# Low parts of a recurrent mixer's second low-rank matrices, from 64 rows to 128 rows with zeros below

## The chip, the core and the metric

One core of a Trainium2 chip runs the whole program. The metric is the device time of one execution in microseconds; for the kernel before it is the median of three executions.

## The reference, cut to what matters

The reference is a trunk of two layers on 256 context and 512 latent tokens of width 1024. Layer 0 is a linear recurrent mixer, layer 1 a recurrent mixer with a state matrix per head (16 heads of 64); each is followed by a mixture of 64 experts. The change is in layer 1. There the decay and the step size of every channel come from two low-rank products, in both directions z:

```
def _rwkv_prep(u, mu, w_in, w0, w_l1, w_l2, a0, a_l1, a_l2, ...):
    ...
    d_w = w0 + einsum('zbtl,zld->zbtd', tanh(einsum('btd,zdl->zbtl', xm[3], w_l1)), w_l2)
    w = exp(-RWKV_DECAY_SCALE * sigmoid(d_w))
    a = sigmoid(a0 + einsum('zbtl,zld->zbtd', einsum('btd,zdl->zbtl', xm[4], a_l1), a_l2))
    ...
```

The inner rank l is 64. `w_l2` and `a_l2` are the second low-rank matrices, 64 x 1024 each for the two directions.

## The kernel before, in words

Layer 1's mixer is the method `rwkv`. Its first stage computes keys, receptances, the gate and the hidden activations of the two low-rank products. The second stage, where the change lies, goes over eight channel blocks `j` of 128 channels (two heads). It runs from about 1600 us to 2475 us of the span.

Numbers are carried as pairs of parts, hi and lo, in the type fp32r, whose sum is the fp32 value. The hidden activations `hid[n][z]` (n is "w" or "a") are tiles of 128 rows by 768 tokens: rows 0 to 63 hold the hi part of the 64 hidden values, rows 64 to 127 the lo part. For each block, `loads` (L1429) fetches the 64 x 2 x 128 slices of the second matrices, and `key` (L1440) splits them: the hi part is written by ScalarE (L1447) into both halves of a tile of 128 rows, the lo part by VectorE (L1448) into a tile of 64 rows. In `a0` (L1465) each of six units (direction z, group g of 256 tokens) then makes for "w" and for "a" one pair of TensorE products of 256 columns: L1474 takes hi against all 128 rows of `hid` (that is hi times hi plus hi times lo), and L1475 adds lo against the 64 upper rows (lo times hi). The tile is called `l_ps` in the trace, the matrices `l2w` and `l2a`. Eight blocks, six units and two matrices give 96 such pairs. ScalarE reads each result with a tanh (L1476).

After `a0` come `a1` to `a5`: elementwise work, the score products `sc_ps` (L1535, 64 rows each, the two heads in rows 0 to 63 and 64 to 127) and the transposes `bt_ps` (L1568, 128 rows). `solver`, `inverse` and `merge` invert small triangular systems, with products of 32 x 32 (`pz`, L1631 and L1636). `chain` (L1647) is the recurrence itself: in twelve chunks, in both directions, `c0` (L1683), `c1` (L1697) and `c2` (L1708) form a serial loop from TensorE to ScalarE or VectorE and back, with products `pg` of 128 rows by 64 columns; `po` (L1718, L1720) gives the outputs. Beside it run the value projection of the blocks (`vproj`, `vp_ps`, L1343, 128 x 128), and the modulation of the next layer (`ada_ps`, L362).

The work of all blocks is put into one list of timed events (`at`, L1793, with the table SCH) and the closures are called in that order. The order on each engine is not that of the calls alone: the program is opened with `tile.TileContext(nc, schedule_with_timeline_sim=True)`, so the builder sets the order of instructions on each engine by a simulated timeline. TensorE takes its instructions strictly in the order that is set.

Of the kernel before, what the change touches and what calls it, by code (L numbers as in the profile page):

```python
# [9 lines left out]
F32 = mybir.dt.float32  # L10
F32R = mybir.dt.float32r
# [3 lines left out]
OP = mybir.AluOpType  # L15
# [256 lines left out]
class Kern:  # L272
# [789 lines left out]
    def rwkv(self, first, done, prepare, res):  # L1062
        nc, ins, tc = self.nc, self.ins, self.tc
# [4 lines left out]
        with ExitStack() as st:  # L1068
# [28 lines left out]
            hid = {n: [fr.tile([128, NTOK], F32R, name=f"hid{n}{z}") for z in range(2)] for n in "wa"}  # L1097
# [6 lines left out]
            with ExitStack() as s1:  # L1104
# [18 lines left out]
                for t in range(NT):  # L1123
                    h = first(t)
                    ps = psw.tile([128, KD, 128], F32, name="u1_ps", tag="w")
# [47 lines left out]
                def wload(ap, n):  # L1173

                    w = wp.tile([128, KD, n], F32, name="rw_f", tag=f"rwf")
                    self.load(w, ap.rearrange("(k p) n -> p k n", p=128))
                    hl = [wp.tile([128, KD, n], F32R, name=f"rw{s}", tag=f"rw{s}") for s in range(2)]
                    for k in range(0, KD, 2):
                        self.split(hl[0][:, k:k + 2], hl[1][:, k:k + 2], w[:, k:k + 2])
                    return hl  # L1180

                def proj_t(w, x, t0):

                    ps = psw.tile([128, 2, 512], F32, name="pt_ps", tag="w")
                    for k in range(KD):
                        for a, b in ((0, 0), (0, 1), (1, 0)):
                            for s, s0, n in SEGS:
                                if s0 >= t0:
                                    nc.tensor.matmul(ps[:, s, :n], w[a][:, k, :], x[k][b][:, s0:s0 + n],  # L1189
                                                     start=(k == 0 and a == 0 and b == 0), stop=(k == KD - 1 and a == 1))  # L1190
                    return ps
# [33 lines left out]
                for j in range(KD):  # L1225
                    w = wload(ins["rwkv_w_in"][0, 1][:, j * 128:(j + 1) * 128], 128)
                    ps = proj_t(w, x, 0)
# [21 lines left out]
                for j in range(KD):  # L1249
                    w = wload(ins["rwkv_w_in"][0, 0][:, j * 128:(j + 1) * 128], 128)  # L1250
                    ps = proj_t(w, x, NCTX)
# [5 lines left out]
                w = wload(ins["rwkv_g_l1"][0], 128)  # L1257
                ps = proj_t(w, x, NCTX)
# [9 lines left out]
                for t in range(NLAT // 128):  # L1268
                    ps = psw.tile([128, 2, 512], F32, name="gg_ps", tag="w")
                    for c in range(2):  # L1270
                        for n, (a, b) in enumerate(((0, 0), (0, 1), (1, 0))):
                            nc.tensor.matmul(ps[:, c, :], ghs[a][:, t * 128:(t + 1) * 128], g2s[b][:, c * 512:(c + 1) * 512],
                                             start=(n == 0), stop=(n == 2))
# [9 lines left out]
            with ExitStack() as s2:  # L1283
                b2 = sf.enter_context(self.pool(name="r2", bufs=1))
                pp = sf.enter_context(self.pool(name="r2_p", bufs=2))
# [143 lines left out]
                def loads(j, P):  # L1429
# [6 lines left out]
                    for n in "wa":  # L1436
                        w = P["l2f"][n] = pp.tile([64, 2, 128], F32, name=f"l2{n}", bufs=1)
                        self.load(w, ins[f"rwkv_{n}_l2"][0][:, :, J].rearrange("z l d -> l z d"))

                def key(j, P):  # L1440
                    P["l2"] = {}
                    for n in "wa":
                        w = P["l2f"][n]
                        hi = pp.tile([128, 2, 128], F32R, name=f"l2{n}0", bufs=1)
                        lo = pp.tile([64, 2, 128], F32R, name=f"l2{n}1", bufs=1)
                        for b in range(2):
                            nc.scalar.activation(hi[r64(b)], w, AF.Copy)  # L1447
                        nc.vector.tensor_tensor(lo, w, hi[:64].bitcast(F32), op=OP.subtract)  # L1448
                        P["l2"][n] = hi, lo

                    kk = P["kk"] = pp.tile([128, NTOK], F32, name="kk")
                    q = PO["kk"] + j
                    for s, t0, n in SEGS:
                        ps = psg.tile([128, 512], F32, name="kk_ps", tag="g")
                        nc.tensor.matmul(ps[:, :n], indT[:, j, :], rn[:, t0:t0 + n], start=True, stop=True)
                        nc.vector.scalar_tensor_tensor(kk[:, t0:t0 + n], P["kT"][:, t0:t0 + n], pc[:, q:q + 1], ps[:, :n], op0=OP.mult, op1=OP.mult)
                    P["kts"] = pp.tile([128, NLAT], F32, name="kts", bufs=1)

                    P["n_d"] = dp.tile([96, 32, 32], F32, name="n_d", bufs=4)
                    P["z_d"] = dp.tile([96, 32, 32], F32, name="z_d", bufs=4)  # L1460
                    P["no"] = wk.tile([128, NCH, 32], F32, name="no", bufs=BUF["no"])
# [3 lines left out]
                def a0(j, P, z, g):  # L1465
                    U = P[z, g] = {}
                    G = slice(256 * g, 256 * g + 256)
                    ps = psg.tile([128, 2, 256], F32, name="l2_ps", tag="g")
                    U["w"] = wk.tile([128, 256], F32, name="uw")
                    U["a"] = wk.tile([128, 256], F32, name="ua")  # L1470
                    for i, n in enumerate("wa"):
                        col = (i * 2 + z) * KD + j
                        hi, lo = P["l2"][n]
                        nc.tensor.matmul(ps[:, i, :], hi[:, z, :], hid[n][z][:, G], start=True, stop=False)  # L1474
                        nc.tensor.matmul(ps[:, i, :], lo[:, z, :], hid[n][z][:64, G], start=False, stop=True)  # L1475
                        nc.scalar.activation(U[n], ps[:, i, :], AF.Tanh, scale=0.5, bias=hb[:, col:col + 1])  # L1476

                def a1(j, P, z, g):
# [325 lines left out]
                for j in range(KD):  # L1804
                    P, t = {}, j * SCH["per"] + SCH["sh"][j]
                    at(t + SCH["ld"], lambda j=j, P=P: loads(j, P))
                    at(t + SCH["key"], lambda j=j, P=P: key(j, P))
                    for u, (z, g) in enumerate(UNITS):
                        for s, f in enumerate((a0, a1, a2, a3, a4, a5)):
                            at(t + SCH["a"] + SCH["du"] * u + SCH["ds"] * s, lambda f=f, a=(j, P, z, g): f(*a))  # L1810
                    t += SCH["off"][j]
                    so = solver(j, P)
                    for i, f in enumerate(so):
                        at(t + SCH["so"] + i * SCH["dso"], f)
                    at(t + SCH["so"] + 1, lambda j=j, P=P: bonus(j, P))
                    for z in range(2):
                        at(t + SCH["inv"] + z * 0.3, lambda a=(j, P, z): inverse(*a))
                    for i, (z, g) in enumerate(UNITS):
                        at(t + SCH["mo"][i], lambda a=(j, P, z, g): merge(*a))
                    b, c = chain(j, P)  # L1820
                    at(t + SCH["bt"], b)
                    for i, f in enumerate(c):
                        at(t + i, f)
                    for f, d in zip(readout(j, P), SCH["ro"]):
                        at(t + 36 + d, f)
# [14 lines left out]
                i = 0  # L1840
# [294 lines left out]
```

## Time and profile before

| | us |
|---|---|
| median of three executions | 3397.05 |
| lowest, highest | 3382.0, 3406.42 |
| the profiled execution | 3397.3 |
| its span, first to last instruction | 3395.5 |
| stage of the change, in the span | about 1600 to 2475 |

A row of the profile names an engine (PE is TensorE's products, PEld its weight loads, DVE VectorE, ACT ScalarE, POOL GpSimd), a line of the kernel, an operation and its tiles, out<-in. For TensorE "64\*128 64x256" means weights of 64 rows by 128 columns and a moving operand of 64 rows by 256 columns. The ends of products are modelled, starts are recorded, so the time a product takes of TensorE is read from its start to the next start. [...]

### The profile page before, as it was taken

How to read it: one execution, taken by the hardware profiler on the slowest of the kernel's cores; microseconds unless marked ns; L12 is line 12 of the kernel's file. 1: busy time of each engine (PE TensorE's matmuls, PEld its weight loads, DVE VectorE, ACT ScalarE, POOL GpSimd, SP SyncE). 2: the span in 40 equal slices, each digit the busy share in tenths (PEclk: the TensorE clock that was granted, in tenths of full speed). 3: DMA queues.
4: the chain of work that ended last, by engine and by line, in shares of the span. 5: the costliest groups of instructions: out<-in, count | busy, mean ns of one | idle time of the engine just before them, and what ended most of it. 6: DMA issues, size and time to landing. Idle time of an engine off the chain costs nothing. (4 is left out here: it accounts for less than half of the span.)

```text
span 3395.5 us, 52648 instructions
## 1 busy us (share of the span) xinstructions
PE 2976.2 (88%) x17929; PEld 2076.3 (61%) x17929; DVE 2403.6 (71%) x4728; ACT 2006.7 (59%) x3835; POOL 1125.8 (33%) x1341
## 2 busy tenths in 40 slices
PE   7998768899999998498989998999877898899993
PEld 3665756667676665376757776767655665555551
DVE  4555557788878887767774756765554888789886
ACT  2664335667766776666645454654333676677773
POOL 0323002333333433122544455543421232333331
PEclk9998879999999999699975678577977999899997
DMA  6446339999999998433675666566524999999995
GB/s 218 126 133 195 116 147 271 307 318 333 339 292 322 330 314 283 137 105 125 152 192 147 176 186 184 147 185 169 171 97 172 320 327 330 309 353 356 344 341 175
DMA packets 329665, 784.71 MB, mean 231 GB/s; under 512 B 129176, under 2 KB 194008, under 8 KB 279856
## 3 DMA queue, kind: packets, MB, share of 16 engines
q1 hardware_dynamic: 276576, 668.36, 59.5%
q0 software_dynamic: 52816, 112.93, 13.9%
q8 instruction: 145, 2.38, 0.3%
q14 instruction: 128, 1.05, 0.1%
HBM read 644.66 MB, written 134.82 MB: 230 GB/s over the span
## 5 line engine op out<-in xcount | busy, mean ns | idle before, releaser
L95 PE MATMUL ph<-w1s,xs 128*128 128x512 f32 (+21 forms) x3216 | 808.1, 401 | 5.6 <-ACT xs L305 2.7
L308 DVE TENSOR_TENSOR w1s<-w,w1s 128x1024 fp32r<-128x1024 f32 x516 | 609.1, 1221 | 67.5 <-ACT w1s L305 66.7
L95 PEld LDWEIGHTS ph<-w1s,xs 128*128 128x128 f32 (+21 forms) x3216 | 490.6, 157 | 247.3 <-DVE xs L308 13.1
L1034 POOL DMA_INDIRECT acc_d<-yt,ix x150 | 303.9, 2026 | 949.3 <-ACT yt L141 312.5
L305 ACT ACTIVATE w1s<-w 128x1024 fp32r<-128x1024 f32 x516 | 516.8, 1057 | 5.3 <-DMA w<-in_moe_w_gu_dram 4.9
L95 PE MATMUL py<-w2s,hT 128*128 128x512 f32 (+22 forms) x1608 | 428.6, 417 | 38.4 <-DVE yt L138 25.5
L95 PEld LDWEIGHTS py<-w2s,hT 128*128 128x128 f32 (+22 forms) x1608 | 250.5, 163 | 160.4 <-issue 34.1
L305 ACT ACTIVATE xs<-px 128x512 fp32r<-128x512 f32 (+23 forms) x287 | 131.2, 457 | 358.8 <-DVE xs L308 224.8
L308 DVE TENSOR_TENSOR w2s<-w,w2s 128x1024 fp32r<-128x1024 f32 x258 | 303.6, 1217 | 8.1 <-ACT w2s L305 8.1
L305 ACT ACTIVATE w2s<-w 128x1024 fp32r<-128x1024 f32 x258 | 258.3, 1053 | 13.2 <-DMA w<-in_moe_w_down_dram 13.1
L308 DVE TENSOR_TENSOR xs<-px,xs 128x512 fp32r<-128x512 f32 (+23 forms) x287 | 146.4, 510 | 157.3 <-ACT xs L305 157.3
L932 POOL DMA_INDIRECT xg<-u_d,ix x150 | 215.8, 1438 | 89.1 <-issue 42.2
L141 ACT ACTIVATE yt<-py 128x512 f32<-128x512 f32 (+20 forms) x282 | 151.6, 593 | 45.6 <-PE py L95 25.7
L73 PE MATMUL px<-ident,xg 128*128 128x128 f32 (+25 forms) x1224 | 129.6, 249 | 44.8 <-DMA xg<-u_d,ix 44.8
L73 PEld LDWEIGHTS px<-ident,xg 128*128 128x128 f32 (+25 forms) x1224 | 111.2, 144 | 68.8 <-issue 61.0
L1690 POOL TENSOR_TENSOR SU<-SU,pC 64x128 f32<-64x128 f32 x176 | 96.6, 554 | 154.2 <-DVE SU L1710 130.9
L542 PE MATMUL in_ps<-uT,w_in 128*128 128x256 f32 (+1 forms) x768 | 143.3, 344 | 4.1 <-ACT w_in L305 2.1
L1189 PE MATMUL pt_ps<-xm,rw 128*128 128x256 f32 (+1 forms) x600 | 130.0, 370 | 14.3 <-ACT xm L305 7.9
L542 PEld LDWEIGHTS in_ps<-uT,w_in 128*128 128x128 f32 x768 | 118.6, 189 | 35.1 <-ACT w_in L305 6.4
L1535 PE MATMUL sc_ps<-X,uBK 64*128 64x128 f32 (+1 forms) x768 | 133.6, 358 | 0.7 <-POOL upt L1494 0.6
L1189 PEld LDWEIGHTS pt_ps<-xm,rw 128*128 128x128 f32 x600 | 102.1, 192 | 45.4 <-ACT xm L305 9.2
L1535 PEld LDWEIGHTS sc_ps<-X,uBK 64*128 64x128 f32 x768 | 113.3, 253 | 21.1 <-issue 8.4
(461 smaller groups left out, 5578.0 us busy)
## 6 DMA issues: line engine op xcount, KB each, us to landing
w<-in_moe_w_gu_dram SPq DMA_DIRECT2D x256, 1024.0 KB
w<-in_moe_w_down_dram SPq DMA_DIRECT2D x128, 1024.0 KB
ada_w<-in_ada_w_dram SPq DMA_DIRECT2D x96, 512.0 KB
O<-op SPq DMA_DIRECT2D x32, 768.0 KB
op<-NN SPq DMA_DIRECT2D x48, 256.0 KB
op<-NN SPq DMA_DIRECT2D x32, 384.0 KB
SU<-v_d SPq DMA_DIRECT2D x48, 256.0 KB
acc_d<-zrow SPq DMA_DIRECT2D x17, 512.0 KB
```

The source lines that it names most:

```text
L73: self.nc.tensor.transpose(px[:, k, :C], x[:C, k * 128:(k + 1) * 128], self.K.ident[:C, :C])
L95: self.nc.tensor.matmul(out[:C], x[a][:, :C], w[b], start=(first and a + b == 0), stop=(last and a == 1))
L141: self.nc.scalar.activation(yt[:C, c * 512:(c + 1) * 512], py[:C, c, :], AF.Copy)
L305: nc.scalar.activation(hi, src, AF.Copy)
L308: (lo_eng or nc.vector).tensor_tensor(lo, src, hi.bitcast(F32), op=OP.subtract)
L542: nc.tensor.matmul(ps[:, s, :n], whl[a][:, k, :], uT[b][:, k, t0:t0 + n], start=(k == 0 and a == 0 and b == 0), stop=(k == KD - 1 and a == 1))
L932: nc.gpsimd.indirect_dma_start(out=x[:C], out_offset=None, in_=u_d, in_offset=bass.IndirectOffsetOnAxis(ap=IW[blk][0], axis=0))
L1034: nc.gpsimd.indirect_dma_start(out=acc_d[n % 2], out_offset=bass.IndirectOffsetOnAxis(ap=ix, axis=0), in_=yt[:C], in_offset=None, compute_ ...
L1189: nc.tensor.matmul(ps[:, s, :n], w[a][:, k, :], x[k][b][:, s0:s0 + n], start=(k == 0 and a == 0 and b == 0), stop=(k == KD - 1 and a == 1))
L1535: nc.tensor.matmul(sc[h][:, c, :nr, :], BK[r64(h), c].rearrange("p a t -> p (a t)"), X[r64(h), :, c, :], start=True, stop=True)
L1690: nc.gpsimd.tensor_tensor(SV[z, g2][r64(0), :, k2], S[r64(0), :, k], P[z, g]["pC"][:, k].to_broadcast([64, 2, 64]), op=OP.mult)
```

## The change

One tile of 128 rows per matrix, kept for all blocks, takes the place of the 64-row tile of each block. Its lower 64 rows are set to zero once, by four VectorE instructions (identity times 0.0); `key` writes only the upper 64 rows. L1475 then takes all 128 rows of weights and of `hid`, so the lower rows add zero. The lines after it move down by seven.

```diff
+                LO = {}
+                for n in "wa":
+                    LO[n] = b2.tile([128, 2, 128], F32R, name=f"l2{n}1")
+                    for z in range(2):
+                        nc.vector.tensor_scalar(LO[n][64:, z], self.ident[64:], 0.0, None, op0=OP.mult)
+
                 def key(j, P):
...
                         hi = pp.tile([128, 2, 128], F32R, name=f"l2{n}0", bufs=1)
-                        lo = pp.tile([64, 2, 128], F32R, name=f"l2{n}1", bufs=1)
+                        lo = LO[n]
                         for b in range(2):
                             nc.scalar.activation(hi[r64(b)], w, AF.Copy)
-                        nc.vector.tensor_tensor(lo, w, hi[:64].bitcast(F32), op=OP.subtract)
+                        nc.vector.tensor_tensor(lo[:64], w, hi[:64].bitcast(F32), op=OP.subtract)
...
                         nc.tensor.matmul(ps[:, i, :], hi[:, z, :], hid[n][z][:, G], start=True, stop=False)
-                        nc.tensor.matmul(ps[:, i, :], lo[:, z, :], hid[n][z][:64, G], start=False, stop=True)
+                        nc.tensor.matmul(ps[:, i, :], lo[:, z, :], hid[n][z][:, G], start=False, stop=True)
```

The builder's timeline sets another order with it, inside this stage only: on TensorE, VectorE, ScalarE, GpSimd and the DMA queue of SyncE the order is that of before ahead of the stage and behind it. The first place on TensorE where the order differs lies about 770 products behind the first pair, in the first block's recurrence. Before, TensorE had there (`bt_ps` transposes, `sc_ps` scores, `pg` the recurrence, `l_ps` the pair):

```order
L1708 MATMUL pg_17426<-SU_17250,O_17252 64x64 x2
L1683 MATMUL pg_17545<-SU_17245,O_17247 64x64 x2
L1568 MATMUL bt_ps<-ident,uBK 128x128
L1535 MATMUL sc_ps<-X_17355,uBK 128x128 x3
L1568 MATMUL bt_ps<-ident,uBK 128x128
L1535 MATMUL sc_ps<-X_17355,uBK 128x128
L1568 MATMUL bt_ps<-ident,uBK 128x128 x2
L1535 MATMUL sc_ps<-X_17355,uBK 128x128 x4
L1683 MATMUL pg_17550<-SU_17250,O_17252 64x64
L1474 MATMUL l_ps<-hida_13340,l2a_16401 128x256
L1475 MATMUL l_ps<-hida_13340,l2a_16402 128x256
L1683 MATMUL pg_17550<-SU_17250,O_17252 64x64
```

In the changed kernel the same place on TensorE reads (lines seven higher, so L1482 is the low product):

```order
L1715 MATMUL pg_17426<-SU_17250,O_17252 64x64 x2
L1690 MATMUL pg_17545<-SU_17245,O_17247 64x64 x2
L1575 MATMUL bt_ps<-ident,uBK 128x128
L1542 MATMUL sc_ps<-X_17355,uBK 128x128 x4
L1575 MATMUL bt_ps<-ident,uBK 128x128 x2
L1542 MATMUL sc_ps<-X_17355,uBK 128x128 x4
L1575 MATMUL bt_ps<-ident,uBK 128x128
L1690 MATMUL pg_17550<-SU_17250,O_17252 64x64 x2
L1704 MATMUL pg_17545<-g_17011,ZT_17015 64x64 x2
L1481 MATMUL l_ps<-hida_13340,l2a_16402 128x256
L1482 MATMUL l_ps<-hida_13340,l2a_15245 128x256
```

The transposes and scores stand in fewer, longer runs, the two `pg` products of L1683 are no longer parted by the pair, and a step of the recurrence (L1697, now L1704) comes ahead of the pair.

The second place is VectorE at the start of the stage, where the zeros are written (`ka`, `hb`: constants of the stage; `vw`: weights of the value projection; `kk`: keys). The rows of the changed kernel:

```order
L1311 TENSOR_SCALAR hb<-rcol 128x32
L1313 TENSOR_SCALAR ka<-rcol 128x8
L1445 TENSOR_SCALAR l2w_15242<-ident 64x128 x2
L1445 TENSOR_SCALAR l2a_15245<-ident 64x128
L1314 TENSOR_SCALAR ka<-ka 128x8
L1445 TENSOR_SCALAR l2a_15245<-ident 64x128
L308 TENSOR_TENSOR vw_15819<-vw_f,vw_15818 128x256
L1463 SCALAR_TENSOR_TENSOR kk<-kT,rcol,kk_ps 128x256
```

Before, the same rows stood there without the four of L1445; nothing else moves at this place.

## Rows read from the trace of the kernel before

**Rows 1.** The page: busy time by engine, and the granted clock in 40 slices.
```profile
PE 2976.2 (88%) x17929; PEld 2076.3 (61%) x17929; DVE 2403.6 (71%) x4728; ACT 2006.7 (59%) x3835; POOL 1125.8 (33%) x1341
...
PEclk9998879999999999699975678577977999899997
```

**Rows 2.** Busy time by stretch: the stage's start, its middle, the whole stage.
```profile
core 0: us, PE busy (x) PEld busy (x) DVE busy (x) ACT busy (x) POOL busy (x), PEclk, DMA share, GB/s
1600.00:1745.00 145.00, 126.99 (x803) 98.71 (x803) 110.16 (x249) 83.55 (x231) 77.52 (x147) 0.92 0.67 161
1745.00:2245.00 500.00, 475.86 (x4118) 349.46 (x4117) 317.64 (x828) 276.08 (x857) 241.19 (x484) 0.66 0.65 171
...
1600.00:2475.00 875.00, 809.11 (x6973) 599.99 (x6971) 553.33 (x1415) 445.82 (x1368) 416.51 (x774) 0.75 0.64 168
```

**Rows 3.** Waits in the stage, 1600 to 2475 us: total, times, longest.
```profile
DVE SU L1710 <- PE pg L1708: 91.0, 76, 6.6
...
PE pg L1697 <- DVE g L1685: 11.3, 16, 3.4
PE pg L1683 <- DVE SU L1710: 7.2, 12, 1.6
PE pg L1708 <- ACT SU L1698: 6.8, 16, 1.3
```

**Rows 4.** Timeline of TensorE around one pair: start, length, what.
```profile
1910.41 0.56 PE L1474 MATMUL l_ps<-hidw,l2w 128*128 128x256 f32 x1
1910.91 0.58 PE L1475 MATMUL l_ps<-hidw,l2w 64*128 64x256 f32 x1
1911.42 0.58 PE L1708 MATMUL pg<-SU,O 128*64 128x64 f32 x3
```

**Rows 5.** The same view around another pair.
```profile
1884.89 0.38 PE L1474 MATMUL l_ps<-hidw,l2w 128*128 128x256 f32 x1
1885.20 0.38 PE L1475 MATMUL l_ps<-hidw,l2w 64*128 64x256 f32 x1
1885.51 0.33 PE L1568 MATMUL bt_ps<-ident,uBK 128*128 128x128 f32 x1
```

**Rows 6.** Busy time and granted clock of the two stretches of rows 4 and 5.
```profile
1884.80:1886.00 1.20, 1.20 (x9) 0.74 (x7) 0.88 (x3) 0.38 (x1) 0.33 (x1) 1.00 1.01 270
1910.00:1911.60 1.60, 1.60 (x8) 1.08 (x7) 0.00 (x0) 1.46 (x5) 0.59 (x1) 0.50 1.08 228
```

**Rows 7.** Timeline of TensorE: a pair between products of the value projection.
```profile
1614.33 0.28 PE L1474 MATMUL l_ps<-hida,l2a 128*128 128x256 f32 x1
1614.54 0.38 PE L1475 MATMUL l_ps<-hida,l2a 64*128 64x256 f32 x1
1614.85 2.38 PE L1343 MATMUL vp_ps<-xm,vw 128*128 128x256 f32 x12
1617.06 0.28 PE L1474 MATMUL l_ps<-hida,l2a 128*128 128x256 f32 x1
```

**Rows 8.** The weight loads of the same stretch.
```profile
1614.53 0.18 PEld L1475 LDWEIGHTS l_ps<-hida,l2a 64*128 64x128 f32 x1 [0.25 <-issue]
1614.84 2.06 PEld L1343 LDWEIGHTS vp_ps<-xm,vw 128*128 128x128 f32 x12
```

**Rows 9.** Timeline of TensorE: the three low products that follow one another.
```profile
1605.94 0.62 PE L1475 MATMUL l_ps<-hidw,l2w 64*128 64x256 f32 x3
1606.48 0.38 PE L1474 MATMUL l_ps<-hidw,l2w 128*128 128x256 f32 x1
```

**Rows 10.** Groups by line, engine and form, 1600 to 2475 us: count, busy us, mean ns.
```profile
L1475 PE MATMUL l_ps<-hida,l2a 64*128 64x256 f32 x48 | 22.9, 477 | 0.0
```

**Rows 11.** Timeline of TensorE: a low product with a score product behind it.
```profile
2040.81 0.58 PE L1475 MATMUL l_ps<-hida,l2a 64*128 64x256 f32 x1
2040.81 1.11 PE L1535 MATMUL sc_ps<-X,uBK 64*128 64x64 f32 x4
```

**Rows 12.** Groups of VectorE by line, 1595 to 1606 us.
```profile
L1303 DVE TENSOR_SCALAR km<-ts 128x64 f32<-128x64 f32 x2 | 0.4, 179 | 0.0
```

## The prediction

> **What bounds the kernel now.** I read the page first, then a table of busy time by stretch, then the waits, then TensorE's timeline. The page gives TensorE the largest busy share, 88% of the span, and shows its clock falling in the middle slices [rows 1]. The table by stretch tells why the stage of the change matters: from 1600 to 2475 us TensorE is busy for 809 of 875 us (92.5%), VectorE for 553, ScalarE for 446, GpSimd for 417, and the mean granted clock is 0.75, with 0.66 in the middle part, where the pairs and the recurrence lie together [rows 2]. Half of the stage thus runs at 1.2 GHz, half at 2.4. The waits say the same: the recurrence's VectorE step sat idle for 91.0 us waiting for TensorE, while TensorE waited for the recurrence's other engines for 11.3 + 7.2 + 6.8 = 25.3 us [rows 3]. TensorE takes its instructions in order and is the bound of this stage. A product made shorter there moves what stands behind it.
>
> **What a pair costs.** At 1.2 GHz the pair takes 1911.42 - 1910.41 = 1.01 us, of which the low product takes 0.51 [rows 4]; at 2.4 GHz it is 1885.51 - 1884.89 = 0.62 us, of which the low product takes 0.31 [rows 5]; the two stretches had granted clocks of 0.50 and 1.00 [rows 6]. A product of the same 256 columns is far cheaper when the neighbours have its shape: twelve products of 128 x 128 weights, six of 256 and six of 512 columns, took 1617.06 - 1614.85 = 2.21 us, which is 18 units of 256 columns at 0.123 us [rows 7]. The difference lies at the change of shape. Behind the 128-row product the load of the 64 rows begins only as the next product's slot begins (1614.53), and the load engine sat idle for 0.25 us before it, though nothing else was due [rows 8]; the next 128-row load in turn waited for the end of the 64-row product. It isn't the 64 rows as such that are slow: where three low products follow one another, all three take 1606.48 - 1605.94 = 0.54 us, so the first two take (0.54 - 0.31) / 2 = 0.115 us each and only the last, before a change of shape, pays [rows 9]. So each change of shape costs, at the product ahead of it, its tail and the load that isn't hidden: 0.31 - 0.123 = 0.187 us at 2.4 GHz. At 1.2 GHz I double the stream to 0.246, and a change costs 0.51 - 0.246 = 0.264 us. The 48 low products of "a" take 477 ns on average by the modelled lengths [rows 10], which lie at 380 and 580 [rows 4, 5]; so 97/200 = 48% of them run at the lower clock, and the mean price is 0.48 x 0.264 + 0.52 x 0.187 = 0.224 us.
>
> **The sum.** I counted changes of shape (rows and columns of the weights) in TensorE's order of the stage, before and after.
> - Between the 96 low products and their neighbours there were 181: 94 ahead of them (two stood behind another low product) and 87 behind. With 128 rows there are none ahead and 64 behind: those followed by a 128 x 128 product (13 of the value projection, 13 transposes, 4 high products, 2 low ones) have none, while seven followed by a score product of 64 rows get one that they hadn't. That is 117 fewer, times 0.224 = 26.2 us.
> - The order that the builder sets has further 35 fewer (973 in all before, 821 after, less the 117): scores and transposes stand in longer runs. Many of these lie at narrower or shorter products, whose change isn't priced by a row above; the bounds are 0 and 35 x 0.224 = 7.8 us. I take 3.5, the middle.
> - A loss: of the seven low products with scores behind them, the score product could start at the same moment (2040.81 both), since the other 64 rows were free [rows 11]. With 128 rows it can't. I count 1 us for these; the whole of seven changed products at 0.123 to 0.246 is 0.9 to 1.7.
> - The four VectorE instructions that write zeros: 4 x 0.179 = 0.7 us by the nearest one of its kind [rows 12]. They stand ahead of the first pair, beside the keys' own work; if all of it delayed the first pair it would cost 0.7, once. The subtraction in `key` keeps its size, and its tile had one buffer before too. I count 0. No DMA is added or taken away.
>
> Together 26.2 + 3.5 - 1 = 28.7 us of TensorE's time. Not all of it reaches the end. Where TensorE stands idle for another engine, a product that became shorter only lengthens the wait, so I take the busy share, 0.925, and get 26.5 us; the bounds are 0.8 (23) and 1 (28.7).
>
> The last term is the clock. A pair at 1.2 GHz takes 1.01 us against 0.62, so a microsecond that turns from the lower level to the upper saves 0.39 us. Half of the stage, some 437 us, is at the lower level. The part with the densest 128 x 128 work (1600 to 1745 us) had 0.92, the middle 0.66 [rows 2], so denser work speaks for a little more of the upper level. A rise or fall of the mean by 0.05 in the 500 us of the middle would be 50 us at the other level, or 20 us of time each way. I take 13 us turned, 5 us saved, and keep -20 and +20 for the range.
>
> The forecast is 3397.3 (the profiled execution, 0.25 us over the median) - 26.5 - 5 = 3365.8, say 3366 us, 0.9% faster.
>
> [...] The loads of twelve 128-row products took 2.06 us beside the 2.21 us of the products [rows 7, 8], so loads of one shape do hide under products of the same rows. [...]
>
> **Rivals.**
> 1. The load stays exposed and only the tail goes. For it: both products of a pair add to the same columns of one accumulation, which the value projection's neighbours don't. Against it: the hidden loads and the three low products in a row [rows 8, 9]. The load's share is the slot of a high product whose load was hidden, 1614.54 - 1614.33 = 0.21 us [rows 7], against one whose load was not, 1885.20 - 1884.89 = 0.31 [rows 5]: 0.10 at 2.4 GHz, and 0.10 to 0.20 at the lower clock. What remains is 0.087 and about 0.115 us, 0.10 on average, and 117 x 0.10 x 0.925 = 11 us: 3386 us.
> 2. The change doesn't do what it says: the slot isn't set by the shape, but by something that the pair keeps. For it: the pair's low product was never seen here with 128 rows. Against it: the same product in a row of three takes 0.115 [rows 9]. Then only the order moves: 3394 us.
> 3. The other side: the builder's new order delays the recurrence. Each chunk's loop passes through TensorE three times in both directions, and longer runs of scores and transposes stand ahead of a recurrence product; TensorE then comes to it early at other places, and waits. Its place is the three waits of 25.3 us [rows 3]. If they tripled, 51 us would come on top of the forecast: 3417 us. It decides from about 31 us of added waits. For it: the first moved place has runs of four scores unbroken. Against it: the same place brings a recurrence step ahead of a pair and closes a split step, and the recurrence waits for TensorE far more than the other way.
> 4. The clock follows: the denser stream keeps the upper level for longer, the mean of the middle rises by 0.10, and 40 us are saved in place of 5: 3331 us. For it: long stretches of the middle are at the lower level, so there is much to win. Against it: the recurrence's narrow products, which fill most of the middle, stay.
>
> **How the numbers follow.** I give the forecast 0.58, rivals 1 to 4 0.12, 0.10, 0.08 and 0.12. A measurement tells about 1% of this kernel's time, 34 us, from no change, so the line is at 3363 us. The forecast lies 3 us above it with some 20 us to each side from the clock and 8 from the order's price: 0.28 of its 0.58 is faster by over 1%, 0.30 within. Rival 4 adds 0.12 to faster; rivals 1 and 2 fall within 1%; of rival 3's 0.08 I leave 0.06 slower by over 1%, with waits that more than triple, and 0.02 within. That makes 0.40 faster, 0.54 within, 0.06 slower. The range runs from rival 4 (3331) to just above no change (3398), which leaves out most of rival 3 and the far side of rival 4.
>
> **What would show it.** Right, step by step: low products with 128 rows whose slot ahead (the high product's) is 0.21 to 0.32 us at either clock in place of 0.31 to 0.51; pairs beside the value projection taking about 0.25 us in place of 0.52; TensorE's busy time in the stage down by about 29 us with no new waits of `pg`; the stage some 30 us shorter and the rest of the span unchanged. Wrong: high products that still take 0.31 and 0.51 us (rival 2) or pairs that lose only 0.1 us (rival 1); waits of `pg` for VectorE and ScalarE well over 25 us (rival 3); a mean clock of the middle that is off 0.66 by 0.05 or more, which would carry the result by more than the pairs do.

## The result, and the profile after

The changed kernel takes 3346.2 us (median of four executions, 3339.3 to 3361.0), the kernel before 3391.0 (four executions beside them, 3382.0 to 3406.4). The ratio is 0.9865, 95% interval 0.9833 to 0.9898: about 45 us or 1.35% faster. The forecast was 3366 us, 0.9% faster; the time lies inside the range, and past the line of 1%, on the side that had been given 0.40 against 0.54 for within it.

The page of the changed kernel, the lines that answer to [rows 1]:

```profile
PE 2922.9 (88%) x17929; PEld 2049.7 (61%) x17929; DVE 2407.7 (72%) x4732; ACT 2001.2 (60%) x3835; POOL 1137.6 (34%) x1341
...
PEclk9998969999999999699977677678977999999997
```

TensorE has as many products as before and is busy 53 us less, all other engines about as long as before. The digits of the clock in the middle are higher on the whole (7677678 where 5678577 stood). What the prediction calls 2.4 and 1.2 GHz are the granted clocks 1.00 and 0.50 [rows 6], the column PEclk at full and at half; no run shows a clock in GHz.

Busy time by stretch, changed kernel, columns as in [rows 2]; the last row is the stage by its own ends, from the first pair to the last product of `po`:

```profile
1600.00:1745.00 145.00, 124.32 (x861) 101.30 (x861) 112.85 (x257) 85.81 (x239) 76.77 (x144) 0.88 0.69 166
1745.00:2245.00 500.00, 465.19 (x4312) 349.15 (x4311) 336.65 (x863) 282.88 (x885) 257.65 (x505) 0.71 0.68 179
1600.00:2475.00 875.00, 781.44 (x7072) 589.60 (x7071) 584.00 (x1532) 457.76 (x1394) 428.11 (x807) 0.78 0.65 176
...
1604.00:2431.00 827.00, 750.43 (x6958) 568.69 (x6956) 555.33 (x1414) 439.61 (x1364) 411.71 (x771) 0.78 0.66 176
```

And the same stage of the kernel before, by its own ends:

```profile
1605.00:2478.00 873.00, 806.62 (x6962) 597.72 (x6962) 552.11 (x1422) 445.18 (x1367) 415.58 (x785) 0.74 0.63 167
```

The stage fell from 873 to 827 us with the same products in it. Busy time of TensorE fell by 56 us, twice what the pairs can give; its idle time rose from 873 - 806.6 = 66 to 827 - 750.4 = 77 us; and the granted clock rose from 0.74 to 0.78, in the middle from 0.66 [rows 2] to 0.71. Behind the stage the two profiles differ by another 11 us. That part is chance: a second profile of the kernel before has 906.7 us there, where the first had 917.7 and the changed kernel has 906.6, and every other profile of the study lies between 904 and 911.

TensorE's timeline, changed kernel: pairs beside the value projection (answering [rows 7]), one at a granted clock of 0.50 ([rows 4]) and one at 1.00 ([rows 5]):

```profile
1609.88 0.28 PE L1481 MATMUL l_ps<-hida,l2a 128*128 128x256 f32 x1
1610.01 0.28 PE L1482 MATMUL l_ps<-hida,l2a 128*128 128x256 f32 x1
1610.12 2.25 PE L1343 MATMUL vp_ps<-xm,vw 128*128 128x256 f32 x12
...
1913.20 0.58 PE L1481 MATMUL l_ps<-hida,l2a 128*128 128x256 f32 x1
1913.58 0.41 PE L1482 MATMUL l_ps<-hida,l2a 128*128 128x256 f32 x1
1913.93 0.31 PE L1638 MATMUL pz<-sd,no 32*32 32x32 f32 x2
...
2052.39 0.39 PE L1481 MATMUL l_ps<-hida,l2a 128*128 128x256 f32 x1
2052.61 0.28 PE L1482 MATMUL l_ps<-hida,l2a 128*128 128x256 f32 x1
2052.82 0.45 PE L1690 MATMUL pg<-SU,O 128*64 128x64 f32 x4
```

Start to start, a pair beside the value projection takes 0.24 us (0.52 before). With products of another shape around it, it takes 0.73 us at a granted clock of 0.50 (1.01 before) and 0.43 at 1.00 (0.62 before).

The weight loads of the first of these pairs, to set beside [rows 8]:

```profile
1609.88 0.19 PEld L1482 LDWEIGHTS l_ps<-hida,l2a 128*128 128x128 f32 x1
1610.01 2.05 PEld L1343 LDWEIGHTS vp_ps<-xm,vw 128*128 128x128 f32 x12
```

The low product's load now begins with the high product (1609.88), 0.13 us ahead of its own product; before, it began with its own (1614.53 and 1614.54).

Waits of TensorE in the stage, changed kernel, answering [rows 3]:

```profile
PE ada_ps L362 <- DMA ada_w<-in_ada_w_dram: 16.0, 5, 7.5
...
PE pg L1690 <- DVE SU L1717: 10.1, 16, 2.6
PE pg L1704 <- DVE g L1692: 8.0, 16, 2.8
PE pg L1715 <- ACT SU L1705: 7.7, 20, 1.4
```

The three waits of the recurrence sum to 25.8 us, against 25.3 before.

### The profile page after: what moved, and what is told of

Its sections match the earlier page's. It is cut to its first block, busy times and chain, and to the rows that moved or that the text cites. A ratio compares the mean times of both kernels' runs of the same rounds, so it can differ in the third digit from the quotient of the medians.

```text
span 3337.8 us, 52624 instructions
## 1 busy us (share of the span) xinstructions
PE 2922.9 (88%) x17929; PEld 2049.7 (61%) x17929; DVE 2407.7 (72%) x4732; ACT 2001.2 (60%) x3835; POOL 1137.6 (34%) x1341
## 5 line engine op out<-in xcount | busy, mean ns | idle before, releaser
L1034 POOL DMA_INDIRECT acc_d<-yt,ix x150 | 316.0, 2107 | 924.3 <-ACT yt L141 376.6
L73 PE MATMUL px<-ident,xg 128*128 128x128 f32 (+25 forms) x1224 | 130.1, 250 | 25.1 <-DMA xg<-u_d,ix 25.1
L1697 POOL TENSOR_TENSOR SU<-SU,pC 64x128 f32<-64x128 f32 x176 | 88.3, 505 | 144.6 <-DVE SU L1717 111.2
L362 PE MATMUL ada_ps<-ada_w,sS 128*32 128x512 f32 x384 | 102.7, 698 | 24.6 <-DMA ada_w<-in_ada_w_dram 24.4
```

Of the source, the lines that this page charges most:

```text
L73: self.nc.tensor.transpose(px[:, k, :C], x[:C, k * 128:(k + 1) * 128], self.K.ident[:C, :C])
L362: nc.tensor.matmul(PS[ch][q], self.sS[:, k, :], w[:, k - kh, :], start=(k < 4), stop=(k >= KD - 4))
L1034: nc.gpsimd.indirect_dma_start(out=acc_d[n % 2], out_offset=bass.IndirectOffsetOnAxis(ap=ix, axis=0), in_=yt[:C], in_offset=None, compute_ ...
L1697: nc.gpsimd.tensor_tensor(SV[z, g2][r64(0), :, k2], S[r64(0), :, k], P[z, g]["pC"][:, k].to_broadcast([64, 2, 64]), op=OP.mult)
```

## The experiments

Two things changed at once: the shape of 96 products, and the order that the builder set. The builder's order changes with nearly every edit, so in six kernels it was pinned: the order of another kernel was read for each engine, and neighbours in it were tied by dependencies that order instructions and carry no wait.

```diff
+                for e, o in ORD.items():
+                    q = seq[e]
...
+                    for p, k in zip(o, o[1:]):
+                        tc.add_manual_dep(q[k], q[p].name, mybir.DependencyInfo(mybir.DependencyClass.NoSync, mybir.DependencyReason.DATA), reason="order")
```

`seq` holds each engine's instructions as the code issues them, `ORD` their places in the order wanted. Kernels that ran together share the executions of the kernel before; "clock" is the mean granted clock over the whole span and over the executions. The changes of shape are counted from the first pair to the last product of `po`, two fewer than in the forecast's count for both kernels.

| kernel | median us | ratio to before, 95% | clock | changes of shape in the stage |
|---|---|---|---|---|
| before (23 executions) | 3392.5 | | 0.8751 | 971 |
| new_shape_old_order | 3360.3 | 0.9895, 0.9853 to 0.9937 | 0.8850 | 854 |
| w_only_old_order | 3373.5 | 0.9962, 0.9929 to 0.9994 | 0.8791 | 909 |
| old_shape_new_order | 3369.5 | 0.9926, 0.9899 to 0.9952 | 0.8816 | 936 |
| changed_again | 3353.7 | 0.9883, 0.9842 to 0.9924 | 0.8833 | 819 |
| before (17 executions) | 3396.6 | | 0.8752 | 971 |
| grouped_64_rows | 3383.1 | 0.9972, 0.9942 to 1.0002 | 0.8757 | 878 |
| changed_po_128_rows | 3350.0 | 0.9881, 0.9841 to 0.9920 | 0.8887 | 613 |
| changed_po_128_grouped | 3308.9 | 0.9762, 0.9722 to 0.9802 | 0.8947 | 567 |
| before (11 executions) | 3394.4 | | 0.8743 | 971 |
| grouped_128_rows | 3360.2 | 0.9892, 0.9855 to 0.9929 | 0.8828 | 812 |
| numbers_for_zeros | 3362.7 | 0.9905, 0.9874 to 0.9936 | 0.8817 | 854 |
| changed_grouped | 3348.3 | 0.9848, 0.9811 to 0.9884 | 0.8890 | 798 |

**Shape without order: new_shape_old_order.** The changed kernel in the order of the kernel before.

> The low products have 128 rows, as in the changed kernel, but every engine's instructions in the stage stand in the order of the kernel before. Theory 'shape' (the gain is the 117 changes of shape that go, 0.224 us each, and what the clock adds): 24 to 40 us faster than before, ratio 0.988 to 0.993, high products' slots of about 0.22 us at 2.4 GHz in place of 0.31. Theory 'order' (the builder's new order brings most of it): within 12 us of before, ratio 0.9965 to 1. Theory 'sum of both': about half of the change's 45 us.

Measured 0.9895 (32 us, inside what theory 'shape' gave), at a higher clock than before. Its stage, in the same view:

```profile
1608.00:2453.00 845.00, 765.25 (x6963) 577.08 (x6961) 557.41 (x1414) 438.37 (x1364) 420.74 (x781) 0.77 0.65 172
```

Since the order is the same, each of the 6962 products can be set beside its twin, start to next start. The table sums the differences in us; the last column gives the noise, from two profiles of one program.

| products | before, to new shape in old order | old shape in new order, to changed_again | the same, to the changed kernel's first profile | before, to before_again |
|---|---|---|---|---|
| the 192 low-rank products | -24.5 | -20.3 | -22.8 | -0.5 |
| others, same clock level in both | -1.4 | -0.2 | -0.7 | -0.3 |
| others, at another clock level | -15.4 | -4.8 | -25.1 | +10.1 |
| products with a wait | +14.0 | +1.2 | +6.3 | +0.8 |
| sum | -27.3 | -24.1 | -42.3 | +10.1 |

In the old order the pairs gave 24.5 us. Of the 192 products, 164 kept their clock level and saved 18.5, so all would have saved 18.5 x 192/164 = 21.7 at equal clock. Some 2.3 us more stand among the others at the same clock level, in slots behind a low product that now has its neighbour's shape: 13 of the value projection, 0.10 us shorter each, and ten transposes, 0.09 each. Waits took 14.0 back: TensorE's idle time rose from 66 to 845 - 765.3 = 80 us. No one wait holds this. The largest part is a DMA; the recurrence's products and small waits share the rest:

```profile
PE ada_ps L362 <- DMA ada_w<-in_ada_w_dram: 17.3, 7, 8.1
...
PE pg L1704 <- DVE g L1692: 10.7, 19, 1.8
PE pg L1690 <- DVE SU L1717: 8.9, 16, 1.9
PE pg L1715 <- ACT SU L1705: 7.0, 17, 1.3
PE pg L1704 <- ACT g L1692: 6.3, 12, 3.6
```

The first and the last of these in the kernel before:

```profile
PE ada_ps L362 <- DMA ada_w<-in_ada_w_dram: 12.3, 5, 8.1
...
PE pg L1697 <- ACT g L1685: 4.0, 11, 1.4
```
The waits answer to all that became shorter, by the clock too: 27.3 of 24.5 + 1.4 + 15.4 = 41.3 us reached the end of the stage. In the new order it was 24.1 of 25.3 and 42.3 of 48.6 us.

**Order without shape: old_shape_new_order.** The kernel before in the order of the changed one.

> The kernel before (64-row low products) with every engine's instructions in the stage in the order of the changed kernel. Theory 'shape': 0 to 10 us faster than before (35 changes of shape fewer between other products). Theory 'order': 30 to 45 us faster, ratio 0.987 to 0.991. Theory 'order hurts' (the forecast's third rival, hidden by a larger gain): 5 us slower or more.

Measured 0.9926 (23 us), between what the theories gave: the order alone makes the kernel faster, by more than its 35 changes were to bring and by less than the whole gain, also at a higher clock. Its profiled execution was the slowest of its twelve, at 3392.7 us against a median of 3369.5, with a clock of 0.873 where the mean was 0.8816; the granted clock of its stage is 0.75, hardly above before:

```profile
1611.00:2481.00 870.00, 802.31 (x6962) 596.75 (x6962) 551.68 (x1418) 443.49 (x1366) 410.55 (x783) 0.75 0.64 168
```

One profile would have said that the order does next to nothing. The twelve times say otherwise.

Shape and order don't add up. By the means of the spans the shape alone gave 3389.9 - 3354.0 = 36 us and the order alone 3389.9 - 3368.3 = 22, but both together 3389.9 - 3350.7 = 39 (changed_again, which ran beside them). Once the new order is there, the rows bring another 18 us, and the clock moves only from 0.8816 to 0.8833.

**Half the dose: w_only_old_order.** Only the matrix of "w" gets 128 rows, in the old order.

```diff
-                for n in "wa":
+                for n in "w":
...
-                        lo = LO[n]
+                        lo = LO[n] if n in LO else pp.tile([64, 2, 128], F32R, name=f"l2{n}1", bufs=1)
```

> Half a dose: only the matrix of the decay gets 128 rows, the other keeps 64, in the order of the kernel before. Theory 'shape': half of what the run with both matrices and the old order gains, 12 to 20 us, ratio 0.994 to 0.9965. A theory in which one particular place or a threshold of the clock decides: either all of that gain or none.

Measured 0.9962 (19 us between the medians, 13 by the ratio), as theory 'shape' gave: between a third and six tenths of the whole shape's gain, and the clock (0.8791) has gone 40% of the way from 0.8751 to 0.8850. In the old order time and clock go with the number of 128-row pairs, as far as three points tell.

**The changed kernel once more: changed_again.**

> The changed kernel once more, beside the three others on one chip. All theories: ratio 0.983 to 0.990 to before. Theory 'the 11 us behind the stage are chance': the stretch from the last recurrence product to the end is within 6 us of 918 us in this profile; if the change does something there it is 907 again.

Measured 0.9883. Its profile of the stage is 846 us where the first one was 827, with the same program and order; by the trace it has 59 us more at the lower clock level, so 18.2 / 59 = 0.31 us are lost for each microsecond there. Over the 23 executions of the kernel before, the span against the time at the lower level gives 0.35; among the other kernels the highest slope is 0.46 (grouped_64_rows, twelve executions). Behind the stage it has 906.0 us. By the test set above, that would have made the 11 us the change's doing; the second profile of the kernel before, with 906.7, shows that the first one's 917.7 was the odd one.

**Fewer changes, same rows: grouped_64_rows.** 64-row low products as before, but in each unit both high products first, then both low ones, which takes 93 changes of shape away; pinned to the old order otherwise.

```diff
                     for i, n in enumerate("wa"):
...
+                        nc.tensor.matmul(ps[:, i, :], hi[:, z, :], hid[n][z][:, G], start=(i == 0), stop=False)
+                    for i, n in enumerate("wa"):
...
+                        nc.tensor.matmul(ps[:, i, :], lo[:, z, :], hid[n][z][:64, G], start=False, stop=(i == 1))
```

> The kernel before with its 64-row low products, but each unit's four products stand together, the two high ones first and then the two low ones, at the place of the first of them; everything else in the order of the kernel before. 93 changes of shape fewer (878 for 971) without any product of 128 rows more. Theory 'shape' (what counts is the stalls at changes of shape, and the clock follows the denser stream): 93/117 of what new shape in the old order gained, about 25 us, ratio 0.990 to 0.995. Theory 'rows' (the clock rises because more rows of the array are fed): only the part at equal clock, some 5 to 12 us, with the lower clock level held about as long as before.

Measured 0.9972, interval up to 1.0002, clock as before (0.8757): theory 'rows' had it so, and 'shape' missed. Removing 93 changes, where the 128 rows remove 117, gave some 10 us, just within the noise, and no clock. The slots themselves did become shorter: in its profile the 192 low-rank products took 19.6 us less than in the kernel before.

**Then the rows: grouped_128_rows.** The same grouped order, with low products of 128 rows.

> As the run with grouped 64-row products, instruction for instruction in the same order, but the low products have 128 rows: 812 changes of shape for 878. Theory 'shape': 66 fewer, about 8 us faster than that run at an equal clock, and the clock hardly moves, as it didn't for its 93 (mean granted clock of the span 0.8757 there, 0.8752 before). Theory 'rows': the mean granted clock rises as in the other runs with 128 rows, to 0.883 or more, and the run is 20 us or more faster than the 64-row one, ratio to before 0.985 to 0.991.

Measured 0.9892, clock 0.8828. The stages of the two, 64 rows first:

```profile
1606.00:2455.00 849.00, 780.18 (x6962) 585.30 (x6962) 552.03 (x1419) 440.41 (x1366) 415.62 (x786) 0.75 0.65 172
```

```profile
1604.00:2448.00 844.00, 759.84 (x6963) 577.48 (x6961) 548.13 (x1415) 438.24 (x1365) 423.35 (x791) 0.76 0.65 173
```

TensorE is busy 20 us less and idle 844 - 759.8 = 84 in place of 849 - 780.2 = 69 us: in this profile waits took 15 of it back. Over the executions the 128 rows are worth 0.8%, from an order on TensorE that differs in nothing. The two kernels ran beside different executions of the kernel before: against its own, the 64-row one has 0.0005 more clock and the 128-row one 0.0085.

**Numbers in place of zeros: numbers_for_zeros.** In the old order, the lower rows hold 1e-9 times a ramp, so what the chip multiplies there is no longer zero.

```diff
-                        nc.vector.tensor_scalar(LO[n][64:, z], self.ident[64:], 0.0, None, op0=OP.mult)
+                        nc.vector.tensor_scalar(LO[n][64:, z], self.jmp[64:], 1e-9, None, op0=OP.mult)
```

> New shape in the old order, with very small numbers (1e-9 times a ramp) in the lower rows in place of zeros; the lower rows then add about 1e-9 to the sums. If only the shape counts: the same time and clock as with zeros (median 3360, mean clock 0.885), ratio 0.985 to 0.994. If the values fed count for the clock: off by more than 0.005 in the clock and 15 us in the time.

Measured 0.9905 at a clock of 0.8817, against 0.9895 and 0.8850 with zeros: within the noise, numbers of this size do what zeros do.

**The kernel before once more: before_again.**

> The kernel before, once more, for a second profile. If the 918 us behind the stage were chance, this shows 905 to 912; the stage takes 860 to 885 us with 420 to 470 us of it at the lower clock level; high products' slots at the two levels as before.

Measured 3395.7 us. Its stage has 882.5 us where the first profile had 872.4 (472 of it at the lower clock level, against 447), and behind it 906.7 where that had 917.7: a single profile says each of these to some 10 us.

**Towards a better version: changed_po_128_rows, changed_grouped, changed_po_128_grouped.** The same idea at the second product of `po` (L1720 before), which takes 64 rows: four tiles `O` that are kept, with zeros below, and all rows taken.

```diff
+                            nc.gpsimd.memset(x[r64(1), 3], 0.0)
...
-                                    nc.tensor.matmul(po[r64(h)], O[r64(0), 3, h, k], S[r64(0), h, k], start=False, stop=True)
+                                    nc.tensor.matmul(po[r64(h)], O[:, 3, h, k], S[:, h, k], start=False, stop=True)
```

The second of the three is the changed kernel with high and low products grouped, the third has both edits. Each is in the order that the builder gives it.

> The changed kernel, and the same idea at the second output product of the recurrence: its 64 x 64 weights become 128 x 64 with lower rows of zeros (the tiles are kept, the zeros written once), the shape of the products around it. 613 changes of shape for 819, each of a narrow product, some 0.09 us at 2.4 GHz and 0.14 at 1.2; but two 64-row products that could run at once no longer do. Theory 'shape': 206 x 0.11 less 128 x 0.06, about 15 us faster than the changed kernel, more with the clock: ratio to before 0.978 to 0.985. Theory 'recurrence' (the stage is now held by the serial loop): within 5 us of the changed kernel, with the waits of the loop's products up by the time saved.

> The changed kernel with each unit's four products traced as two high and then two low, in an order that the builder sets (798 changes of shape), without the 128-row output product: tells which of the two gave the 37 us by which the run with both was faster than the run with the output product alone. If grouping: 3315 to 3330 us, ratio 0.976 to 0.984. If both are needed, or the builder's order of that one program was a lucky one: 3340 to 3355 us, ratio 0.984 to 0.990.

> The same, and each unit's four products together (two high, then two low): 567 changes of shape. Theory 'shape': another 46 x 0.2, 5 to 10 us faster than the run without the grouping: ratio to before 0.975 to 0.983. Theory 'recurrence': no faster than that run.

Measured 0.9881, 0.9848 and 0.9762. `po` alone took 206 changes of shape away (819 to 613) and gained nothing that shows over the changed kernel (0.9883), as theory 'recurrence' gave: by its trace TensorE was idle for 113 us of the stage. Grouping alone gained at most a little. Both together are the fastest kernel of the study, 3308.9 us, 2.4% under the kernel before:

```profile
1608.00:2403.00 795.00, 684.79 (x6963) 531.71 (x6962) 547.54 (x1411) 436.08 (x1366) 417.09 (x798) 0.81 0.70 183
```

The idle time is still 795 - 684.8 = 110 us, the clock is 0.81. The grouping was to bring 5 to 10 us on top of `po` and came with 37 to 41. Why both together give more than each alone isn't settled: these three were not pinned to one order.

## Why the prediction was right, and where it wasn't

**The mechanism** was right. In these traces a change of shape cost the product ahead of it a tail and the one behind it a load that wasn't hidden, and pairs of equal shape lost both. With neighbours of another shape the high product's slot at a granted clock of 1.00 fell from 0.31 to 0.22 us (its tail) and the low one's from 0.31 to 0.21 (its load); at 0.50 from 0.50 to 0.38 and from 0.51 to 0.35. So the change inside a pair was worth 0.62 - 0.43 = 0.19 us at 1.00 (forecast 0.187) and 1.01 - 0.73 = 0.28 at 0.50 (forecast 0.264, from a stream taken as doubled: 0.246, where the two low products with a 128 x 128 transpose behind them took 0.21 and 0.22 in new_shape_old_order).

One reading behind the price was wrong. The prediction put the whole cost at the product ahead of a change, and read the three low products of [rows 9] as 0.115, 0.115 and 0.31 us. The same view in two narrower windows has their starts:

```profile
1606.16 0.39 PE L1475 MATMUL l_ps<-hidw,l2w 64*128 64x256 f32 x2
1606.28 0.28 PE L1475 MATMUL l_ps<-hidw,l2w 64*128 64x256 f32 x1
```

From 1605.94 by 1606.16 and 1606.28 to 1606.48 the slots are 0.22, 0.12 and 0.20 us: the first pays its load, the last its tail, and only the one in between pays neither. A slot of 0.31 holds half of the change ahead of it and half of the one behind. The price of a whole change comes out the same, 0.19.

**The pairs' sum** was 26.2 less 1 for lost concurrency; the pinned pair of kernels gives 24.5, of it 21.7 at equal clock, and with the 2.3 us in the slots behind 24.0. Right, to about a microsecond. The concurrency term held: in the old order the seven low products with scores behind them took 0.6 us in all before and 2.0 after. Before, five of the seven scores started 3 or 4 ns after their low product, the other two 0.22 and 0.38 us after it; in the changed kernel's own order each of seven started 0.21 to 0.35 us after it. That the free rows let the five start is the author's reading: the profile doesn't say which rows a score takes.

**The zeros** cost nothing that shows: the two writes for "w", 0.22 us each, began at 1597.0 and 1597.1 us, and the first low part above them was written at 1602.5, ahead of the first pair at 1604.

**What passes through** was put at 0.925. Of all that became shorter, 24.1 / 25.3 = 0.95 and 42.3 / 48.6 = 0.87 passed through in the new order, near it. In the old order it is 27.3 / 41.3 = 0.66, below the lower bound of 0.8; the run with numbers in place of zeros, of the same shape and order, has 26.2 / 36.2 = 0.72. The busy share of a stage didn't tell that apart; that it is the room which an order leaves is likely, but not shown.

**The clock** is the term that was mis-sized. The forecast let 13 us turn from the lower level to the upper and saved 5. Over the ten executions of the changed kernel the mean clock was 0.885 and the mean span 3349 us, before 0.8751 and 3390 (23 executions). The clock records of the two profiles, of the kernel before and of the changed one, hold the levels 1.00 and 0.50 alone; taken so for every execution, the time at the lower one is 2 x (1 - clock) x span: 770 against 847 us, so 77 us fewer. Some 10 of these are the pairs' own shortening at the lower level (8 to 10 us in the pinned runs), so about 67 turned. At 0.31 to 0.35 us each this is 21 to 23 of the 41 us; with the highest slope, 0.46, it would be 31. The forecast's price of 0.39 was near. What is left, 18 to 20 us, is less than the 26.5 that the pairs and the order were to bring. That the total came out as near as it did is in part luck, since the two errors go opposite ways. The prediction had named a middle off 0.66 by 0.05 or more as a sign of being wrong; the first profile has 0.71, the second 0.68.

**The order's own term** was 3.5 us, from its 35 fewer changes. Alone, the order gave 23 us by the medians and 22 by the means. Its mean clock was 0.8816 and its mean span 3368 us, so 798 us at the lower level, 49 fewer than before and worth about 16; some 5 us are left for the changes, near the forecast. Nor do the order and the shape add up, as the sum took it. The order moved the clock, and the forecast had priced it without that.

**The rivals.** Rival 1 (the load stays exposed) fell by the load of 128 rows that begins with the high product of 128 rows (1609.88 both) and by the low slot of 0.21 us. Rival 1's 3386 us leaves out the order's 3.5 us, which rival 2's 3394 has, and neither has the clock's 5. Rival 2 (the slot isn't set by the shape) fell by the pairs of 0.24 and 0.43 us. Rival 3 (the order delays the recurrence) fell twice: the recurrence's three waits are 25.8 against 25.3 us, and the order alone is faster. Rival 4 (the clock follows) was half right: the middle rose by 0.05 in the first profile and by 0.02 in the second, not by 0.10, and the clock's share is some 20 to 30 us, not 40.

**What raises the clock** is shown in part. Adding 128-row products in an order that differs in nothing raised it twice, in the old order (0.8751 to 0.8850) and in the grouped one (0.8757 to 0.8828), and half of them by 40% as much; removing changes of shape at 64 rows did not (0.8757). Whether the rows are zeros or numbers of 1e-9 makes no difference clear of the noise. But the new order with 64-row products raised it as well (0.8816), and there the rows added little (0.8833 beside it, 0.885 over all ten executions). So the rows are one way and not the only one, and what the two have in common is open. Which part of that order does it was not tried.

## What to carry to other kernels

Here a short product with fewer rows, between products of 128 rows, cost a tail and a load at its changes of shape, 0.19 us at a granted clock of 1.00 and 0.28 at 0.50 for a change; filling its rows with zeros took that away for the price of four writes, once, of 0.22 us each, and of the scores that had started beside it (1.4 us). Read what a stage gains from three terms apart: the slots themselves, the waits that take some back (pin the order to see them, and don't take the busy share for the part that passes), and the granted clock, which was the largest here (21 to 23 of 41 us by the estimate above). A builder that reorders with every edit makes a second change of each; pin its order before putting a gain down to the edit, and compare many executions, since single profiles of one program differed by 18 us in this stage.

## What the runs showed of the hardware that wasn't expected

- The granted clock followed rows of zeros: 96 low products with 64 more rows raised the mean of the span from 0.875 to 0.885 in the unchanged old order, though they are half a per cent of TensorE's 17929 products. 1e-9 in place of the zeros gave 0.882. In the new order the same rows moved it from 0.8816 to 0.8833 only.
- At a granted clock of 0.50 the slot of 256 columns wasn't double that at 1.00: 0.345 us for a low product with an unlike neighbour behind it, against 0.209 at 1.00, a factor of 1.65; with a high product ahead and a 128 x 128 transpose behind, 0.216 against 0.119, a factor of 1.8 (new_shape_old_order, two and three products).
- The count of rows and columns wasn't all of it: behind a 128 x 128 transpose a high product of the same 128 x 128 took 0.20 to 0.23 us at a granted clock of 1.00 and 0.36 at 0.50 (new_shape_old_order, six and four products), where behind the value projection it took 0.11 to 0.12.
- Taking 206 further changes of shape away (`po`) at an already short stage gave nothing by itself, and TensorE's idle time rose to 113 us; with the grouping it was worth 0.9% (0.9762 against 0.9848), in orders that were not pinned.
